# Alternating PSUM banks and a second room for pair sums in the gate units of a hybrid attention block

## The chip, the cores and the metric

The kernel runs on one core of a Trainium2 chip. The metric is the device time of one execution in microseconds. A profiled execution also gives the span from the first to the last instruction of the program, with every instruction on the five engines: PE (matrix products), DVE (vector), ACT (scalar and activation functions), POOL, and SP, which only issues transfers here.

## The reference

One block, 256 tokens, width 2048, all in fp32. Cut to what matters here:

```python
h = rmsnorm(x, g_mix)
proj = h @ w_in                         # 2048 x 10240
q_sb, k_sb, v_sb, q_ca, k_ca, v_ca, gate_sb, gate_ca = split(proj)
y_sb = stick_breaking_attention(q_sb, k_sb, v_sb)     # 8 heads of 128
y_ca = chunked_relpos_attention(q_ca, k_ca, v_ca, rel_bias)   # 8 heads of 128
merged = sigmoid(gate_sb) * (y_sb @ w_sb_out) + sigmoid(gate_ca) * (y_ca @ w_ca_out)
x = x + merged @ w_mix_out
g, u = split(rmsnorm(x, g_ffn) @ w_ffn_in)
x = x + (silu(g) * u) @ w_ffn_out
x = x + sigmoid(rmsnorm(x, g_ple) @ w_ple_gate) * (p @ w_ple_in)
out = rmsnorm(x, g_final)
```

## The kernel before

**Products in three parts.** Every fp32 operand is split into a rounded part hi and a rest lo = value - hi. A product is the sum of hi x hi, hi x lo and lo x hi, three matrix instructions (lines 276 to 278, function `three`). A weight piece of 256 x 512 comes from memory by one transfer into a place `raw` (five places, `RAW = 5`), ACT casts it to hi (L247), DVE subtracts to get lo (all subtractions are recorded at L229, in `minus`). hi and lo have three buffers each, and a fourth in some stages (`four_buffers`).

**Units.** The function `unit` computes two column blocks of 512 (a double group) over 16 rows of weight tiles. A part of its work goes by a Strassen-like scheme: a pair of row tiles of both blocks, seven triple products in place of eight. For it, DVE forms three more weight matrices `xf` (two from raw, one over it, one more: three different lines of `split_pair`, all at L229), ACT casts the two raw pieces (L262, L265) and xf (L268, into `room`), and DVE subtracts (into lo and `room`). `room` is one tile of 128 x 3072 for hi and lo of xf. The pairs are row pairs 2, 4 and 6 of eight, so a unit is 13 pieces: ten single pieces of 12 products and three pairs of 21. The products go into eight PSUM banks: four main sums (`mm`, one for each block and half of the tokens) and four sums of the pairs (`su`, q1, q5, q6, q7). After the last pair, `mid` writes the four sums into SBUF (an ACT copy at L812, four DVE additions at L814), and after the last pieces `add_sums` adds the main sums (L818).

**Gate units.** In the attention part there are five such units (`gate_unit`): the second half of the values of the first mixer with the first gate block, both halves of the values of the second mixer, and three units of gate blocks. They have `alone=True`: main sums always in the pool `ps_mm` (four banks of 512), pair sums always in the attention pool (two tiles of 1024, the function `aux`), which is also where the attention steps have their scores zp, bt, yp.

**Order.** Pieces are worked off one after another by `flush`; `prefetch` issues loads while places are free and splits up to three pieces ahead. Attention work stands in a queue of tasks: for two heads the steps s1 (scores, exponentials), s2 (sums, weights) and s3 (values). `flush(every)` runs one task after each `every` pieces; in a unit with `hold` no task runs from the first to the last pair. Queries and keys (`queries_and_keys`) are groups of four pieces of 16 products (L354, L356); their two sums leave PSUM through `halves` (ACT copy tm L418, DVE addition sm L420). The program is then put into order per engine by a scheduler, and each engine runs its list in order.

The sequence is: first half of the values and one gate block; queries and keys of mixer 0, half 0; first gate unit (`flush(2)`); queries and keys (0, 1) and (1, 0); the other four gate units (`flush(1000)`); queries and keys (1, 1); output projections, mixing, feed-forward, last gate.

Of the kernel before, what the change touches and what calls it, by code (L numbers as in the profile page):

```python
# [9 lines left out]
F32 = mybir.dt.float32  # L10
# [26 lines left out]
MIX_PAIRS = (4, 6)  # L37
RAW = 5
# [5 lines left out]
def block_kernel(ctx: ExitStack, tc: tile.TileContext, x, p, w_in, w_sb_out, w_ca_out, w_mix_out,  # L44
# [95 lines left out]
    pieces = []  # L140
    tasks = deque()
# [22 lines left out]
    def unit(wsrc, n0s, kts, lhs, forms, ext, slots, mid, post, needs, row0=0, pairs=PAIRS, alone=False, after=None,  # L164
             hold=False):
# [8 lines left out]
        taken = [j for j in pairs if j < len(kts) // 2 - 1]  # L174
        for i in range(len(kts) // 2):
# [4 lines left out]
            if i in taken:  # L180
                pieces.append(dict(pc, src=src, pair=True, first=i == taken[0], last=i == taken[-1]))
            else:
                for b in range(2):
                    pieces.append(dict(pc, src=[src[b]], block=b, first=i == 0, last=2 * i + 2 == len(kts)))
# [5 lines left out]
    def load_piece(src, ncol):  # L190
        state["ring"] += 1
        if state["more"] is not None and state["ring"] % (RAW + MORE) in (0, RAW // 2 + 1):
            raw = state["more"]()
        else:
            raw = wp.tile([P, 1024], F32, tag="raw", name="raw", bufs=RAW)
        n = src.shape[1] * ncol
        return raw[:, :n], raw[:, :n].rearrange("p (k n) -> p k n", n=ncol)

# [32 lines left out]
    def split(pc):  # L231
# [4 lines left out]
        state["raw"] -= len(raws)  # L236
        if pc["g"]["kind"] == "unit" and len(raws) == 2:
            return split_pair(pc, *raws)
# [44 lines left out]
    def pair_products(pc):  # L283
# [25 lines left out]
        if z:  # L309
            g["mid"](g)  # L310
            state["hold"] = False

    def products(pc):
# [3 lines left out]
        elif g["kind"] == "unit":  # L317
            if pc["first"]:
                g["ps"] = g.get("ps", []) + [late["ps"][g["pool"]].tile([P, 512], F32, tag="mm", name=f"mm{t}") for t in range(2)]
# [6 lines left out]
            if pc["last"]:  # L326
                g["post"](g, pc["block"])
        elif pc is pieces[1]:
# [34 lines left out]
    state = dict(loaded=0, split=0, at=0, raw=0, hl=0, ext=0, ps=ps_mm, fourth=None, ring=0, more=None, hold=False)  # L363
# [6 lines left out]
    def prefetch():  # L370
        while state["loaded"] < len(pieces) and state["raw"] + len(pieces[state["loaded"]]["src"]) <= RAW + (MORE if state["more"] is not None else 0):
            load(pieces[state["loaded"]])
            state["loaded"] += 1
# [24 lines left out]
    def flush(every=1, until=None, in_turn=False):  # L398

        n = 0  # L400
        while state["at"] < len(pieces) and (until is None or until not in done):
# [5 lines left out]
            if tasks and not state["hold"] and int(n / every) > int((n - 1) / every):  # L407
# [7 lines left out]
    def halves(ps, pool):  # L415

        tm = pool.tile([P, S], F32, tag="tm", name="tm", bufs=2)
        nc.scalar.copy(tm, ps[:, S:])  # L418
        sm = pool.tile([P, S], F32, tag="sm", name="sm", bufs=2)
# [198 lines left out]
    gates = ap.tile([P, NT, 2, D], F32, tag="gates", name="gates", bufs=1)  # L618

# [98 lines left out]
    def ca_tasks(qT, kT, v, h0):  # L718
# [5 lines left out]
        def s1(h):  # L724
            bias = ap.tile([P, 2, 256], F32, tag="bias", name="bias")
# [120 lines left out]
    F_gate = [FP[:, 0], FP[:, 1], room[:, 3072:].rearrange("p (c f s) -> p c f s", c=2, f=4)]  # L846
    work = mp.tile([P, 1024], F32, tag="v1", name="work")
    state["work"] = lambda name: work[:, :512] if name == "af" else work[:, 512:]
    for i, pair in enumerate(PAIRS):
# [6 lines left out]
              add_values((0, 1)), True)  # L856
    flush(2)
# [10 lines left out]
              add_values((1, 0), (1, 1)), True)  # L868
    for c in range(1, 4):
        gate_unit([6 * W + m * D + c * NB for m in range(2)], lambda c=c: gate_slots(c), add_sums, True)  # L870
    flush(1000)
# [103 lines left out]
    state["more"] = lambda: lp.tile([P, 1024], F32, tag="raw", name="raw", bufs=MORE)  # L975
# [190 lines left out]
```

## Time and profile before

| | us |
|---|---|
| median of three runs | 1473.09 (1472.67 to 1473.83) |
| the profiled execution | 1474.41 |
| its span | 1472.7 |
| PE busy | 1452.7 |
| DVE busy | 1242.6 |
| ACT busy | 820.4 |

A matrix instruction is shown from the start of its reading to a modelled end, so neighbours overlap: of 128 x 512 they start 0.23 us apart and are shown as 0.39. An engine's idle time ahead of an instruction is put down to the one whose end released it. The granted clock is given as a share of the full one.

### The profile page before, as it was taken

How to read it: one execution, taken by the hardware profiler on the slowest of the kernel's cores; microseconds unless marked ns; L12 is line 12 of the kernel's file. 1: busy time of each engine (PE TensorE's matmuls, PEld its weight loads, DVE VectorE, ACT ScalarE, POOL GpSimd, SP SyncE). 2: the span in 40 equal slices, each digit the busy share in tenths (PEclk: the TensorE clock that was granted, in tenths of full speed). 3: DMA queues.
4: the chain of work that ended last, by engine and by line, in shares of the span. 5: the costliest groups of instructions: out<-in, count | busy, mean ns of one | idle time of the engine just before them, and what ended most of it. 6: DMA issues, size and time to landing. Idle time of an engine off the chain costs nothing.

```text
span 1472.7 us, 18664 instructions
## 1 busy us (share of the span) xinstructions
PE 1452.7 (99%) x6849; PEld 1211.8 (82%) x6849; DVE 1242.6 (84%) x1570; ACT 820.4 (56%) x967; POOL 23.0 (2%) x44
## 2 busy tenths in 40 slices
PE   9999999989999999999999999999999999999997
PEld 7887788868888888888888888888888888888886
DVE  6868766888886767898999999899999999999775
ACT  6546656556555544555555545556554556565552
POOL 0200000000000000000000000000000000000000
PEclk9999999999999999999999999999999999999999
DMA  9765455556676556765666666666666666656671
GB/s 320 260 205 172 153 183 168 182 165 207 200 232 204 167 171 183 221 211 172 188 201 199 186 216 198 200 213 187 201 198 201 204 188 207 214 188 213 229 230 69
DMA packets 164731, 291.17 MB, mean 198 GB/s; under 512 B 9024, under 2 KB 42096, under 8 KB 164384
## 3 DMA queue, kind: packets, MB, share of 16 engines
q1 hardware_dynamic: 162528, 281.32, 61.5%
q0 software_dynamic: 2112, 8.68, 1.7%
q8 instruction: 53, 0.87, 0.3%
q14 instruction: 38, 0.31, 0.1%
HBM read 284.19 MB, written 5.77 MB: 197 GB/s over the span
## 4 chain that ended last, share of the span: by engine, by line
PE 94%; ACT 2%; DVE 2%; DMA 1%; issue 1%; DVEq 0%; SPq 0%; ACTq 0%
PE mm L277 22%; PE mm L278 22%; PE mm L276 22%; PE mm L354 7%; PE su L277 4%; PE su L278 4%; PE su L276 4%; PE mm L356 4%; PE tp L443 1%; DVE lo L229 1%; ACT hi L247 1%; DMA raw<-in_w_in 1%; DMA raw<-in_w_ple_in 0%; PE mm L344 0%; DVE room L229 0%
## 5 line engine op out<-in xcount | busy, mean ns | idle before, releaser
L229 DVE TENSOR_TENSOR lo<-raw,hi 128x1024 fp32r<-128x1024 f32 (+1 forms) x517 | 626.4, 1219 | 139.9 <-ACT hi L247 125.1
L247 ACT CAST hi<-raw 128x1024 fp32r<-128x1024 f32 (+1 forms) x387 | 404.7, 1050 | 394.8 <-PE mm L278 294.7
L277 PE MATMUL mm<-lo,T 128*128 128x512 f32 x1349 | 527.0, 391 | 0.2 <-DVE lo L229 0.2
L278 PE MATMUL mm<-hi,T 128*128 128x512 f32 x1349 | 522.9, 390 | 0.0
L276 PE MATMUL mm<-hi,T 128*128 128x512 f32 x1349 | 498.7, 392 | 5.6 <-DVE v L818 3.6
L276 PEld LDWEIGHTS mm<-hi,T 128*128 128x128 f32 x1349 | 253.2, 188 | 59.3 <-issue 4.0
L277 PEld LDWEIGHTS mm<-lo,T 128*128 128x128 f32 x1349 | 253.7, 188 | 53.0 <-DVE lo L229 1.0
L278 PEld LDWEIGHTS mm<-hi,T 128*128 128x128 f32 x1349 | 253.7, 188 | 52.3
L354 PE MATMUL mm<-T,hi 128*128 128x512 f32 x512 | 180.0, 398 | 1.6 <-ACT hi L247 1.6
L356 PE MATMUL mm<-T,lo 128*128 128x256 f32 x512 | 140.0, 280 | 0.0
L265 ACT CAST hi<-raw 128x1024 fp32r<-128x1024 f32 x65 | 68.6, 1055 | 85.8 <-DVE raw L229 31.4
L354 PEld LDWEIGHTS mm<-T,hi 128*128 128x128 f32 x512 | 94.8, 188 | 23.0 <-ACT hi L247 2.3
L356 PEld LDWEIGHTS mm<-T,lo 128*128 128x128 f32 x512 | 96.4, 189 | 1.9
L229 DVE TENSOR_TENSOR xf<-raw 128x512 f32<-128x512 f32 x130 | 89.2, 686 | 8.9 <-DMA raw<-in_w_in 2.9
L229 DVE TENSOR_TENSOR T<-xf,T 128x1536 fp32r<-128x1536 f32 x50 | 87.8, 1755 | 7.5 <-ACT T L268 7.4
L262 ACT CAST hi<-raw 128x1024 fp32r<-128x1024 f32 x65 | 68.5, 1053 | 34.6 <-PE mm L278 28.6
L268 ACT CAST T<-xf 128x1536 fp32r<-128x1536 f32 x50 | 74.0, 1479 | 7.4 <-DVE xf L229 6.8
L814 DVE TENSOR_TENSOR C<-su,C 128x512 f32<-128x512 f32 x72 | 47.7, 684 | 0.3
L818 DVE TENSOR_TENSOR C<-mm,C 128x512 f32<-128x512 f32 x72 | 46.8, 683 | 0.0
L229 DVE TENSOR_TENSOR xf<-raw,xf 128x512 f32<-128x512 f32 x65 | 44.6, 686 | 0.4
L229 DVE TENSOR_TENSOR raw<-raw 128x512 f32<-128x512 f32 x65 | 44.5, 685 | 0.2
L229 DVE TENSOR_TENSOR room<-xf,room 128x1536 fp32r<-128x1536 f32 x15 | 26.4, 1757 | 11.2 <-ACT room L268 11.2
(320 smaller groups left out, 1486.5 us busy)
## 6 DMA issues: line engine op xcount, KB each, us to landing
raw<-in_w_ffn_in SPq DMA_DIRECT2D x176, 512.0 KB, 3.9
raw<-in_w_in SPq DMA_DIRECT2D x160, 512.0 KB, 4.2
raw<-in_w_ffn_out SPq DMA_DIRECT2D x88, 512.0 KB, 4.5
raw<-in_w_mix_out SPq DMA_DIRECT2D x32, 512.0 KB, 4.6
raw<-in_w_ple_gate SPq DMA_DIRECT2D x32, 512.0 KB, 4.9
raw<-in_w_sb_out SPq DMA_DIRECT2D x16, 512.0 KB, 3.8
raw<-in_w_ca_out SPq DMA_DIRECT2D x16, 512.0 KB, 3.8
x<-in_x SPq DMA_DIRECT2D x4, 512.0 KB, 10.1
```

Source lines behind the costliest of these rows:

```text
L229: return nc.vector.tensor_tensor(out, a, b, ALU.subtract)
L247: state["cast"] = nc.scalar.copy(hi[:, c : c + m], raw[:, c : c + m])
L262: nc.scalar.copy(h1, raw1)
L265: nc.scalar.copy(h2, raw2)
L268: nc.scalar.copy(xh, xf)
L276: nc.tensor.matmul(ps, xh, hi, start=a, stop=False)
L277: nc.tensor.matmul(ps, xh, lo, start=False, stop=False)
L278: state["mm"] = nc.tensor.matmul(ps, xl, hi, start=False, stop=z)
L354: nc.tensor.matmul(ps, hi[:, i, f], lhs[:, kt, :, :].rearrange("p c s -> p (c s)"), start=a, stop=False)
L356: nc.tensor.matmul(ps[:, :S], lo[:, i, f], lhs[:, kt, 0, :], start=False, stop=z)
L814: nc.vector.tensor_tensor(C[i], q, C[j], ALU.add)
L818: nc.vector.tensor_tensor(g["C"][i], g["ps"][i], g["C"][i], ALU.add)
```

## The change

The change has four parts, all in the attention part.

- A second room. The pair sums of the gate units alternate between `room` and the upper half of T2 (`later_y`), which holds the second mixer's attention results only later.
- Banks exchanged. `alone` is now a pool number that alternates from gate unit to gate unit, beginning with 1. In units of pool 1 (the first, third and fifth) the main sums are in the attention tiles and the pair sums in `ps_mm`; in units of pool 0 as before. The function `banks` hands them out.
- Tasks held. In a gate unit `hold` is set from the first piece to the last, and `flush(None)` runs no task.
- A sixth raw place from the start of the attention part to the output projections. Its 4 KB come from `tm`, `sm` and `bias`, which go from two buffers to one. `held` remembers which places are taken, so that the sixth is used in turn.

`GATE_ORDER` writes the order of the 13 pieces out; it is the order that `unit` had.

```diff
+GATE_PAIRS = (2, 4, 6)
+GATE_ORDER = (0, 0, 1, 1, -2, 3, 3, -4, 5, 5, -6, 7, 7)
...
+def banks(g, pool, name, n):
+    if g["hold"] and pool == 1:
+        return [t[:, o : o + 512] for t in (aux(name) for _ in range(n // 2)) for o in (0, 512)]
+    return [late["ps"][pool].tile([P, 512], F32, tag="mm", name=f"{name}{t}") for t in range(n)]
...
-        if not alone:
+        if alone is None:
             state["unit"] = state.get("unit", -1) + 1
-        pool = 0 if alone else state["unit"] % 2
+        pool = state["unit"] % 2 if alone is None else alone
...
-                 side=None if alone else 1 - pool, hold=hold)
+                 side=1 - pool, hold=alone is not None)
...
-        if state["more"] is not None and state["ring"] % (RAW + MORE) in (0, RAW // 2 + 1):
+        more = held.count(True) < state["places"] and (
+            held.count(False) == RAW or state["ring"] % (RAW + state["places"]) in (0, RAW // 2 + 1)[: state["places"]])
+        held.append(more)
+        if more:
             raw = state["more"]()
...
-            state["hold"] = g["hold"]
-            if g["side"] is None:
-                su = [aux(f"su{i}") for i in range(2)]
-                g["sums"] = [t[:, o : o + 512] for t in su for o in (0, 512)]
-            else:
-                g["sums"] = [late["ps"][g["side"]].tile([P, 512], F32, tag="mm", name=f"su{i}") for i in range(4)]
+            g["sums"] = banks(g, g["side"], "su", 4)
...
-            state["hold"] = False
...
             if pc["first"]:
-                g["ps"] = g.get("ps", []) + [late["ps"][g["pool"]].tile([P, 512], F32, tag="mm", name=f"mm{t}") for t in range(2)]
+                state["hold"] = g["hold"]
+                g["ps"] = g.get("ps", []) + banks(g, g["pool"], "mm", 2)
...
             if pc["last"]:
                 g["post"](g, pc["block"])
+                state["hold"] = g["hold"] and pc["block"] == 0
...
-            if tasks and not state["hold"] and int(n / every) > int((n - 1) / every):
+            if tasks and every and not state["hold"] and int(n / every) > int((n - 1) / every):
...
-        tm = pool.tile([P, S], F32, tag="tm", name="tm", bufs=2)
+        tm = pool.tile([P, S], F32, tag="tm", name="tm", bufs=1)
-        sm = pool.tile([P, S], F32, tag="sm", name="sm", bufs=2)
+        sm = pool.tile([P, S], F32, tag="sm", name="sm", bufs=1)
...
+    more_places(lambda: ap.tile([P, 1024], F32, tag="raw", name="raw", bufs=1), 1)
...
-            bias = ap.tile([P, 2, 256], F32, tag="bias", name="bias")
+            bias = ap.tile([P, 2, 256], F32, tag="bias", name="bias", bufs=1)
...
-    def gate_unit(n0s, slots, post, hold):
-        unit(w2, n0s, range(KD), T1, lambda kt: F_gate[kt // 4 - 1], [room[:, :3072]], slots, mid, post, hneed,
-             alone=True, hold=hold)
+    def gate_unit(n0s, slots, post):
+        pool = state["gate"] = 1 - state.get("gate", 0)
+        unit(w2, n0s, range(KD), T1, lambda kt: F_gate[GATE_PAIRS.index(kt // 2)], [room[:, :3072], later_y[:, :3072]],
+             slots, mid, post, hneed, alone=pool, order=GATE_ORDER)
...
+    later_y = T2.rearrange("p k c s -> p (k c s)")[:, KD * S :]
...
-    flush(2)
+    flush(None)
...
-    flush(1000)
+    flush(None)
...
+        state["places"] = 0
         flush(2.67 if m == 0 else 1)
```

How the change moves instructions is seen at three places. The lines of the changed kernel are higher: L229 is L250, L247 is L270, L559 is L578, L692 and L693 are L712 and L713, L814 and L818 are L834 and L838, L887 is L909, L608 is L627, L651 and L652 are L671 and L672.

The first is DVE at the start of the first gate unit; zp are the scores of the first two heads, raw_1174 (before) and raw_1146 (now) the first raw piece of the unit's first pair, xf its sums. Before:

```order
L625 TENSOR_TENSOR kT_686<-sm_1105,rbc_87 128x256
L692 SCALAR_TENSOR_TENSOR ls_1127<-zp_1114,e_1123 128x768
L229 TENSOR_TENSOR lo_1209<-raw_1174,hi_1208 128x1024
L693 SCALAR_TENSOR_TENSOR e_1123<-zp_1114,e_1123 128x768
L229 TENSOR_TENSOR room_683<-xf_1207,room_683 128x1536
```

Now:

```order
L712 SCALAR_TENSOR_TENSOR ls_1127<-zp_1114,e_1123 128x768
L645 TENSOR_TENSOR kT_686<-sm_1105,rbc_87 128x256
L250 TENSOR_TENSOR lo_1200<-raw_1146,hi_1199 128x1024
L713 SCALAR_TENSOR_TENSOR e_1123<-zp_1114,e_1123 128x768
L250 TENSOR_TENSOR T2_72<-xf_1198,T2_72 128x1536
```

The row of kT now stands behind the first zp row, and the first pair's rest goes into T2; zp's bank is now wanted by the unit's main sums.

The second is ACT at the end of the first gate unit; v and gates are where `mid` and `add_sums` write, zp_1468 and e_1477 belong to the step s1 of the next two heads. Before:

```order
L812 COPY v_1440<-su0_1277 128x512
L247 CAST hi_1520<-raw_1508 128x1024
L247 CAST hi_1524<-raw_1510 128x1024
L559 ACTIVATE v_1440<-v_1440,r1_mix_89 128x512
L688 ACTIVATE e_1477<-zp_1468 128x768
L559 ACTIVATE v_1440<-v_1440,r1_mix_89 128x512
L689 ACTIVATE e_1477<-e_1477 128x768
L887 ACT_TABLE_LOAD
L887 ACTIVATE gates_518<-gates_518,r1_mix_89 128x512
L690 ACT_TABLE_LOAD
L690 ACTIVATE e_1477<-e_1477 128x768
L887 ACT_TABLE_LOAD
```

Now:

```order
L832 COPY v_1412<-su0_1247 128x512
L270 CAST hi_1462<-raw_1450 128x1024
L270 CAST hi_1136<-raw_1305 128x1024
L270 CAST hi_1466<-raw_1452 128x1024
L270 CAST hi_1470<-raw_1454 128x1024
L578 ACTIVATE v_1412<-v_1412,r1_mix_89 128x512 x2
L909 ACT_TABLE_LOAD
L909 ACTIVATE gates_518<-gates_518,r1_mix_89 128x512 x2
L270 CAST hi_1498<-raw_1456 128x1024
```

The three steps of e with their tables have left this place; casts and one table load are what remains.

The third is DVE at the change from the second to the third gate unit; su_2561 and su_2562 are the two tiles of pair sums, mm0_2472 (before) and mm0_2476 (now) a main sum, and xf is the first pair of the third unit. Before:

```order
L229 TENSOR_TENSOR lo_2449<-raw_2707,hi_2448 128x1024
L814 TENSOR_TENSOR v_2733<-su1_2562,v_2732 128x512
L229 TENSOR_TENSOR xf_2821<-raw_2765 128x512
L814 TENSOR_TENSOR v_2732<-su1_2562,v_2733 128x512
L818 TENSOR_TENSOR v_2732<-mm0_2472,v_2732 128x512
L229 TENSOR_TENSOR raw_2765<-raw_2765,raw_2763 128x512
L229 TENSOR_TENSOR lo_2770<-raw_2689,hi_2769 128x1024
L814 TENSOR_TENSOR v_2733<-su0_2561,v_2732 128x512
L814 TENSOR_TENSOR v_2733<-su0_2561,v_2733 128x512
```

Now:

```order
L250 TENSOR_TENSOR xf_2823<-raw_2741 128x512
L250 TENSOR_TENSOR raw_2741<-raw_2741,raw_2739 128x512
L250 TENSOR_TENSOR xf_2823<-raw_2741 128x512
L250 TENSOR_TENSOR xf_2823<-raw_2739,xf_2823 128x512
L834 TENSOR_TENSOR v_2733<-su_2562,v_2732 128x512
L834 TENSOR_TENSOR v_2732<-su_2562,v_2733 128x512
L838 TENSOR_TENSOR v_2732<-mm0_2476,v_2732 128x512
L834 TENSOR_TENSOR v_2733<-su_2561,v_2732 128x512
L834 TENSOR_TENSOR v_2733<-su_2561,v_2733 128x512
```

The whole of the pair's xf now stands ahead of the additions, and the five additions follow each other. Before, the third unit's first products needed the bank of mm0_2472; now they need the tile su_2561. On PE nine products stand between the last into su_2562 and the third unit's first.

More of the change, by code (lines that the diff above doesn't have):

```diff
@@ L140, in block_kernel @@
     pieces = []
+    held = deque()
     tasks = deque()
@@ L162, in group, with unit @@
             ))
-    def unit(wsrc, n0s, kts, lhs, forms, ext, slots, mid, post, needs, row0=0, pairs=PAIRS, alone=False, after=None,
-             hold=False):
-        if not alone:
+    def unit(wsrc, n0s, kts, lhs, forms, ext, slots, mid, post, needs, row0=0, pairs=PAIRS, alone=None, after=None,
+             order=None):
+        if alone is None:
             state["unit"] = state.get("unit", -1) + 1
-        pool = 0 if alone else state["unit"] % 2
+        pool = state["unit"] % 2 if alone is None else alone
         g = dict(kind="unit", post=post, mid=mid, slots=slots, after=after, lhs=lhs, keep=None, forms=forms, ext=ext, pool=pool,
-                 side=None if alone else 1 - pool, hold=hold)
+                 side=1 - pool, hold=alone is not None)
         kts = list(kts)
-        taken = [j for j in pairs if j < len(kts) // 2 - 1]
-        for i in range(len(kts) // 2):
+        if order is None:
+            order = [j for i in range(len(kts) // 2) for j in ([-i] if i in pairs and i < len(kts) // 2 - 1 else [i, i])]
+        taken = [-i for i in order if i < 0]
+        begun = set()
+        for i in order:
+            own = i < 0
+            i = abs(i)
             part = kts[2 * i : 2 * i + 2]
@@ L236, in split @@
         state["raw"] -= len(raws)
+        for _ in raws:
+            held.popleft()
         if pc["g"]["kind"] == "unit" and len(raws) == 2:
@@ L361, in group_products @@
             g["ps"] = None
-    state = dict(loaded=0, split=0, at=0, raw=0, hl=0, ext=0, ps=ps_mm, fourth=None, ring=0, more=None, hold=False)
+    state = dict(loaded=0, split=0, at=0, raw=0, hl=0, ext=0, ps=ps_mm, fourth=None, ring=0, places=0, hold=False)
     late = dict(ps=[ps_mm])
@@ L370, in prefetch @@
     def prefetch():
-        while state["loaded"] < len(pieces) and state["raw"] + len(pieces[state["loaded"]]["src"]) <= RAW + (MORE if state["more"] is not None else 0):
+        while state["loaded"] < len(pieces) and state["raw"] + len(pieces[state["loaded"]]["src"]) <= RAW + state["places"]:
             load(pieces[state["loaded"]])
```

21 lines of the change are left out of this document (12 added, 9 removed).

## The prediction

> **What bounds the kernel now.** I began with the busy shares on the page, then cut the span into stages, then asked in each stage what PE waited for. PE is the bound:
>
> ```profile
> PE 1452.7 (99%) x6849; PEld 1211.8 (82%) x6849; DVE 1242.6 (84%) x1570; ACT 820.4 (56%) x967; POOL 23.0 (2%) x44
> ```
>
> The change touches only the attention part of the program, so the second view is the busy time by stage. 113 us is the end of the first queries and keys, 113 to 176 the first gate unit, 176 to 255 the next queries and keys, 255 to 434 the end of these and the four other gate units:
>
> ```profile
> core 0: us, PE busy (x) PEld busy (x) DVE busy (x) ACT busy (x) POOL busy (x), PEclk, DMA share, GB/s
> 113.00:176.00 63.00, 58.71 (x275) 46.39 (x275) 48.97 (x62) 42.78 (x48) 0.00 (x0) 1.00 0.51 157
> 176.00:255.00 79.00, 79.00 (x468) 69.61 (x467) 56.09 (x80) 45.45 (x62) 0.00 (x0) 1.00 0.59 182
> 255.00:320.00 65.00, 60.03 (x269) 48.26 (x268) 52.73 (x65) 37.79 (x44) 0.00 (x0) 0.97 0.56 176
> 320.00:434.00 114.00, 114.00 (x505) 94.42 (x504) 98.41 (x103) 67.55 (x67) 0.00 (x0) 1.00 0.65 199
> 434.00:1460.00 1026.00, 1026.00 (x4756) 855.77 (x4755) 899.09 (x1124) 561.06 (x655) 11.51 (x18) 1.00 0.64 197
> ```
>
> PE has no idle time except in the first and third of these rows: 63.00 - 58.71 = 4.3 us and 65.00 - 60.03 = 5.0 us. That is where anything can be won. The waits of PE in these two stretches, 110 to 180 and 255 to 320:
>
> ```profile
> PE mm L354 <- ACT hi L247: 1.6, 2, 1.3
> PE mm L276 <- ACT hi L247: 1.1, 1, 1.1
> PE su L277 <- DVE room L229: 1.1, 1, 1.1
> PE mm L277 <- DVE lo L229: 0.3, 2, 0.2
> PE su L276 <- ACT room L268: 0.2, 1, 0.2
> ...
> PE mm L276 <- DVE v L818: 3.6, 1, 3.6
> PE mm L276 <- ACT hi L247: 0.9, 1, 0.9
> PE su L277 <- DVE room L229: 0.4, 1, 0.4
> ```
>
> The idle time understates the loss. Products start 0.23 us apart though each is shown as 0.39 us long, and the longest wait shows what else goes:
>
> ```profile
> 308.80 0.39 PE L277 MATMUL mm<-lo,T 128*128 128x512 f32 x1
> 309.02 0.39 PE L278 MATMUL mm<-hi,T 128*128 128x512 f32 x1
> 312.98 0.47 PE L276 MATMUL mm<-hi,T 128*128 128x512 f32 x1 [3.57 <-DVE v L818]
> ...
> 313.99 0.61 PE L277 MATMUL mm<-lo,T 128*128 128x512 f32 x1
> 314.39 0.63 PE L278 MATMUL mm<-hi,T 128*128 128x512 f32 x1
> ...
> 317.38 0.41 PE L276 MATMUL mm<-hi,T 128*128 128x512 f32 x1
> ...
> 301.81 0.47 PE L276 MATMUL mm<-hi,T 128*128 128x512 f32 x1
> 302.33 0.50 PE L277 MATMUL mm<-lo,room 128*128 128x512 f32 x1
> 302.67 0.40 PE L278 MATMUL mm<-hi,room 128*128 128x512 f32 x1
> ```
>
> Start to start, the wait at 309 cost 3.96 - 0.23 = 3.7 us. The eight products from 313.99 to 317.38 took 3.39 us where 8 x 0.23 = 1.8 would do, so the slow clock behind it cost 1.6 more. A wait that shows no idle (301.81) cost 0.29 and its restart 0.11. So each of the ten waits counted above costs 0.16 (0.39 - 0.23) and 0.11 more than its idle: 9.3 + 2.7 + 1.6, and about 0.9 for three delays like that at 301.81 (estimate: the other two, at 136.97 and 155.87, taken as alike). In all 14.5 us, 6.8 in the first stretch and 7.7 in the second. This is the most that the change can win here.
>
> **The change part by part.** By the order of instructions, PE, DVE and SP issue as many as before and ACT one table load less. Nothing is saved in work; what moves are waits. Durations for all that follows, from the stretch 320 to 430 in which units follow each other without a wait, then ACT and DVE around the two long waits:
>
> ```profile
> L229 DVE TENSOR_TENSOR lo<-raw,hi 128x1024 fp32r<-128x1024 f32 x43 | 52.5, 1221 | 7.3 <-ACT hi L247 4.4 <-ACT hi L262 1.3 <-ACT hi L265 1.3
> L229 DVE TENSOR_TENSOR room<-xf,room 128x1536 fp32r<-128x1536 f32 x9 | 15.8, 1759 | 7.6 <-ACT room L268 7.6
> L814 DVE TENSOR_TENSOR gates<-su,gates 128x512 f32<-128x512 f32 x8 | 5.3, 686 | 0.5 <-PE su L278 0.4
> ...
> 114.35 0.38 ACT L418 COPY tm<-mm 128x256 f32<-128x256 f32 x1
> 114.66 0.82 ACT L688 ACTIVATE e<-zp 128x768 f32<-128x768 f32 x1
> 115.49 1.28 ACT L689 ACT_TABLE_LOAD   x1
> 116.78 0.85 ACT L689 ACTIVATE e<-e 128x768 f32<-128x768 f32 x1
> 117.65 1.28 ACT L690 ACT_TABLE_LOAD   x1
> 118.95 0.85 ACT L690 ACTIVATE e<-e 128x768 f32<-128x768 f32 x1
> 119.70 1.03 ACT L262 CAST hi<-raw 128x1024 fp32r<-128x1024 f32 x1
> ...
> 309.69 0.68 DVE L814 TENSOR_TENSOR v<-su,v 128x512 f32<-128x512 f32 x1
> 310.94 0.69 DVE L229 TENSOR_TENSOR xf<-raw 128x512 f32<-128x512 f32 x1 [0.56 <-DMA raw<-in_w_in]
> 311.55 0.68 DVE L814 TENSOR_TENSOR v<-su,v 128x512 f32<-128x512 f32 x1
> 312.15 0.68 DVE L818 TENSOR_TENSOR v<-mm,v 128x512 f32<-128x512 f32 x1
> ```
>
> *Tasks held, and banks exchanged, in the first unit.* The attention steps s2, s3 and s1 leave the first unit for the queries and keys behind it. There DVE has 79 - 56.1 = 22.9 us free and ACT 33.6; the steps bring DVE some 9 and ACT some 11 us (estimate: the 128x768 rows at about 0.9, two table loads of 1.28, the rest below 0.7 each), and PE waits nowhere in that row. Cost 0; without that cover it would be the 1.3 us that such a clump of ACT costs at the unit's end now. Inside the unit DVE has per unit 3 pairs x (4 x 0.69 + 2 x 1.22 + 1.76) + 10 x 1.22 + 8 x 0.69 = 38.6 us against PE's (10 x 12 + 3 x 21) x 0.2275 = 41.6. With the steps gone it fits, and with two rooms the next pair's sums need not wait for PE to leave the one room. So the waits from 130 to 176 go.
>
> The unit's start stays, and becomes dearer. Its main sums now take the attention banks, and one of them still holds zp until DVE's second zp addition (L693 before, L713 after). I laid the rows behind each other in the new order, from the end of zp, 114.37: PE has 24 products, to 119.9. ACT does the same six rows as above, with the second tm copy inside, so that Ln ends at 120.05, then hi of the pair until 121.0. DVE's lo of that pair follows kT and ends at 122.5, the second addition at 123.4. PE then goes on after 31 products at 123.8, where it could have been at 121.5: 2.3 us. Lower end 1.0 (the cast of the pair alone late), upper end 3.5 (the second transfer of the pair late as well, as the waits of 0.6 above). I take 2.4. First stretch: 6.8 - 2.4 = 4.4 won.
>
> *Second room and sixth raw place, second stretch.* The waits on room and its neighbours there (0.4 and 0.29, with their 0.27 and 0.11, and two of 0.1) go: 1.3 won. The sixth place issues a transfer one piece, about 2.7 us of products, earlier:
>
> ```profile
> raw<-in_w_in SPq DMA_DIRECT2D x160, 512.0 KB, 4.2
> ```
>
> That takes the 0.56 at 310.94 away. The start of the second unit (0.9 idle, 1.2 in all) keeps its chain: cast, table load, Exp, then the cast that PE needs stand on ACT in the same order. I take 1.3 again, ends 0.5 and 2.6.
>
> *Banks exchanged, change from the second to the third unit.* Before, the third unit's first products waited for L818, with a lo, a wait for DMA and two L814 ahead of it on DVE. After, they take the banks of the four sums and need the last of four L814, with one L818 between. Nine products stand on PE between the last product into the sums and the new unit: 2.0 us. Five DVE instructions at 0.60 (311.55 to 312.15) to 0.69, and some 0.15 each for the two hand-overs by the gaps between rows (estimate), are 3.3 to 3.7. The wait is 1.3 to 1.7; I take 1.6 in place of 3.7, and the slow clock (1.6) and its restart go with the short wait: 3.8 won. Lower end 0.9; upper end 3.6, if the pair's transfer is late again. Behind these DVE instructions stand room and lo of the third unit's first pair, which PE needs 27 products (6.1 us) later; 1.76 + 1.22 fit. At the two later changes PE has 24 to 42 products (5.4 to 9.5 us) against some 5.3 us of DVE; 0 to 1.7 each, I take 0.3 each, 0.6 lost, since DVE is at 86% (98.41 of 114) there.
>
> *Single tm, sm and bias.* The second tm copy of a group waits for the first sm addition. tm is 0.38 and PE's next group has other banks, so I cost it at 0; the cover is the free time of the second stage row.
>
> The sum: 4.4 + 1.3 - 0.1 + 3.8 - 0.6 = 8.8, of which I drop 0.2 for rounding of the small waits: 8.6 us. The profiled execution has 1472.7 of span and takes 1474.41 in all; it would become 1464.1 of span. The median of the runs, 1473.09, is 1.3 below the profiled time, and I predict against it: 1473.1 - 8.6 = 1464.5.
>
> [...] Only the gap of 3.57 us was followed by slow products; with those of 1.3 and 1.1 the granted clock stayed at 1.00 (row 113 to 176). [...]
>
> **The rivals.**
> *B, the waits at the changes of units stay.* Had DVE still to do a late pair there, the wait from 309 would be 3.6 and slow the clock: 1.6 + 2.0 less, and 1.5 at a later change: 8.6 - 5.1 = 3.5 won, 1469.6. For it: DVE's 86%, and the four sums that must all be added. Against: the transfer that was late then comes earlier.
> *C, all covered.* Nothing of the 14.5 is left: 1458.6. Against it: zp is still held at the first unit's start.
> *D, nothing measurable.* DVE, 48.97 of 63 and 52.73 of 65, would set the pace, and waits only change place: 1473. For it: the instructions are the same. Against: DVE itself idles for ACT and rooms while PE waits.
> *E, slower.* tm and sm with one buffer tie ACT to DVE: behind a lo of 1.22 and an sm of 0.42 ACT stands 1.6 us, 16 times. It decides once ACT is later than a piece of a group (2.8 us) with its three buffers; then 16 x 0.8 = 13 us come (half of the stand seen by PE, estimate), less 8.6: 1477. Against: no PE wait between 176 and 255. [...]
>
> **How the numbers follow.** Forecast (1460.5 to 1468.5, from the ends above: start 1.0 to 3.5, change 0.9 to 3.6, second start 0.5 to 2.6) 0.58; B (to 1471) 0.15; C 0.08; D 0.10; E 0.09. A difference of 0.2%, 2.9 us, is about what a measurement of this kernel can tell from no change. Faster than 1470.1: forecast, C and most of B, 0.77. Within 0.2%: D and the rest of B, 0.14; slower, E, 0.09. The range 1459.5 to 1473.0 leaves out half of C, a part of D and E. The likeliest case alone has 1460.5 to 1468.5.
>
> **What would show it.** In the new profile: no wait on room or on L354's cast between 130 and 180; one or two waits near 120 to 124, of 1 to 3.5 us together; one at the change near 305 of about 1.5 with the clock at 1.00; PE's idle in the two stretches at 4 or less. Wrong would be: a new wait on tm, sm or L814 of over 3 us, PE idle between 176 and 255, or losses behind 434.

## The result, and the profile after

The changed kernel takes 1463.48 us (median of nine runs, 1462.98 to 1473.24); the kernel before, run beside it, 1473.83 (1472.07 to 1475.04). The ratio estimated over all runs is 0.9938 (the two medians alone give 0.9930), with a 95% interval of 0.9928 to 0.9949: 7.5 to 10.6 us won. The highest of the nine runs, 1473.24, had a mean granted clock of 0.995; the other eight had 0.997 to 0.999 and lie below 1465.3. Predicted were 1464.5 us. The profiled execution took 1464.04 us, with a span of 1462.3.

First line of the page of the changed kernel, busy time by engine:

```profile
PE 1447.8 (99%) x6849; PEld 1210.3 (83%) x6849; DVE 1242.2 (85%) x1570; ACT 819.6 (56%) x966; POOL 22.5 (2%) x44
```

As many PE instructions as before, and 4.9 us less shown as busy. The same table by stage as in the prediction, for the changed kernel; the later stages begin earlier by about what was won:

```profile
113.00:176.00 63.00, 60.20 (x289) 49.66 (x288) 51.80 (x63) 39.95 (x43) 0.00 (x0) 1.00 0.55 173
176.00:250.00 74.00, 74.00 (x447) 65.50 (x446) 53.76 (x78) 47.56 (x63) 0.00 (x0) 1.00 0.56 168
250.00:313.00 63.00, 61.71 (x290) 51.22 (x290) 57.11 (x68) 40.99 (x46) 0.00 (x0) 1.00 0.58 177
313.00:424.00 111.00, 111.00 (x491) 91.94 (x490) 96.48 (x103) 64.19 (x64) 1.55 (x3) 1.00 0.70 212
```

PE's idle time in the first and third row is 2.8 and 1.3 us, where it was 4.3 and 5.0, and the clock is 1.00 in all rows (0.97 in the third before). What PE waited for between 110 and 320 us, now four waits in all:

```profile
PE mm L299 <- ACT hi L270: 1.3, 1, 1.3
PE mm L300 <- DVE lo L250: 1.2, 1, 1.2
PE su L299 <- ACT hi L285: 0.8, 1, 0.8
PE su L300 <- DVE lo L250: 0.8, 1, 0.8
```

The last three stand at the first unit's start, the first at the second unit's. With 0.27 us for each wait, as in the prediction, they cost 3.6 and 1.6 us: of the 14.5 us that were lost, 5.2 are left, 9.3 won. A second way to the same number: two places with equally many products ahead of them, the first product of the first queries and the first product of a late zp. First the kernel before, then the changed one:

```profile
68.48 0.39 PE L354 MATMUL mm<-T,hi 128*128 128x512 f32 x1
...
473.09 0.28 PE L657 MATMUL zp<-sh 128*128 128x256 f32 x1
```

```profile
67.63 0.39 PE L373 MATMUL mm<-T,hi 128*128 128x512 f32 x1
...
462.06 0.28 PE L677 MATMUL zp<-sh 128*128 128x256 f32 x1
```

The distance between the two is 404.61 us before and 394.43 now: 10.2 us won between them. 0.85 us came ahead of them, where the change does nothing (this place lay between 67.0 and 68.6 us in the kernels below, with the same code ahead of it), and 0.6 was lost behind. Between 9.3 and 10.2, 0.9 us is not traced to a row.

### The profile page after: what moved, and what is told of

Read it like the earlier page. It is cut to its first block, busy times and chain, and to the rows that moved or that the text cites. A ratio compares the mean times of both kernels' runs of the same rounds, so it can differ in the third digit from the quotient of the medians.

```text
span 1462.3 us, 18695 instructions
## 1 busy us (share of the span) xinstructions
PE 1447.8 (99%) x6849; PEld 1210.3 (83%) x6849; DVE 1242.2 (85%) x1570; ACT 819.6 (56%) x966; POOL 22.5 (2%) x44
## 4 chain that ended last, share of the span: by engine, by line
PE 96%; DMA 2%; ACT 1%; DVE 1%; issue 0%; SPq 0%; DVEq 0%; ACTq 0%
PE mm L300 23%; PE mm L301 23%; PE mm L299 23%; PE mm L373 8%; PE su L300 4%; PE su L301 4%; PE su L299 4%; PE mm L375 4%; PE tp L462 1%; DMA raw<-in_w_in 1%; DMA raw<-in_w_ple_in 1%; ACT hi L270 0%; DMA raw<-in_w_mix_out 0%; DVE lo L250 0%; PE yp L689 0%
## 5 line engine op out<-in xcount | busy, mean ns | idle before, releaser
L250 DVE TENSOR_TENSOR lo<-raw,hi 128x1024 fp32r<-128x1024 f32 (+1 forms) x517 | 625.7, 1218 | 131.1 <-ACT hi L270 120.8
L270 ACT CAST hi<-raw 128x1024 fp32r<-128x1024 f32 (+1 forms) x387 | 405.1, 1050 | 399.3 <-PE mm L301 299.0
L250 DVE TENSOR_TENSOR T<-xf,T 128x1536 fp32r<-128x1536 f32 x58 | 101.7, 1754 | 10.4 <-ACT T L291 10.4
L250 DVE TENSOR_TENSOR xf<-raw 128x512 f32<-128x512 f32 x130 | 89.1, 685 | 14.9 <-DMA raw<-in_w_ffn_in 4.2
L291 ACT CAST T<-xf 128x1536 fp32r<-128x1536 f32 x58 | 85.9, 1480 | 18.8 <-DVE xf L250 18.1
L285 ACT CAST hi<-raw 128x1024 fp32r<-128x1024 f32 x65 | 68.5, 1053 | 31.5 <-PE mm L301 24.9
L834 DVE TENSOR_TENSOR C<-su,C 128x512 f32<-128x512 f32 x72 | 47.6, 682 | 0.3
L838 DVE TENSOR_TENSOR C<-mm,C 128x512 f32<-128x512 f32 x72 | 46.6, 680 | 0.0
L250 DVE TENSOR_TENSOR xf<-raw,xf 128x512 f32<-128x512 f32 x65 | 44.5, 685 | 0.4
L250 DVE TENSOR_TENSOR raw<-raw 128x512 f32<-128x512 f32 x65 | 44.5, 684 | 0.2
L301 PE MATMUL mm<-T,T 128*128 128x512 f32 (+1 forms) x90 | 33.4, 371 | 0.0
```

Source lines behind the costliest of these rows:

```text
L250: return nc.vector.tensor_tensor(out, a, b, ALU.subtract)
L270: state["cast"] = nc.scalar.copy(hi[:, c : c + m], raw[:, c : c + m])
L285: nc.scalar.copy(h1, raw1)
L291: nc.scalar.copy(xh, xf)
L301: state["mm"] = nc.tensor.matmul(ps, xl, hi, start=False, stop=z)
L834: nc.vector.tensor_tensor(C[i], q, C[j], ALU.add)
```

## The experiments

Each kernel ran in five rounds beside the kernel before. The interval of a ratio is about 0.0013 to either side, 1.9 us, so the time alone tells two of these kernels apart from some 3 us on; for less, the waits in the profile carry the reading. The column "stretch" is the time between the two places above in each kernel's profile; it leaves out what the program's head adds by chance, but not what the clock does. The last column says what the clock does there: one minus the granted clock, times the time, added up over the stretch in steps of 4 us. It is 0 or 1.7, and 8.5 in run 4. Where the text below gives a stretch "without the clock", this loss is taken off it. A profile is one execution; in how many of the others of a kernel the clock fell is not known, so the times may hold more or less of it.

| kernel | median us | ratio to before (interval) | stretch us | of it lost to the clock, us |
|---|---|---|---|---|
| before | 1473.83 | | 404.61 | 1.7 |
| changed kernel | 1463.48 | 0.9938 (0.9928 to 0.9949) | 394.43 | 0 |
| 1 five places, two buffers | 1461.35 | 0.9919 (0.9905 to 0.9932) | 392.55 | 0 |
| 2 one room | 1467.30 | 0.9955 (0.9942 to 0.9967) | 398.71 | 1.7 |
| 3 banks fixed, 0 0 0 0 0 | 1464.79 | 0.9939 (0.9926 to 0.9951) | 396.18 | 1.7 |
| 4 tasks in the first unit, banks 0 1 0 1 0 | 1477.64 | 1.0026 (1.0015 to 1.0036) | 409.14 | 8.5 |
| 5 five places, single buffers | 1465.86 | 0.9944 (0.9932 to 0.9957) | 396.48 | 1.7 |
| 6 other tile for the third unit | 1464.18 | 0.9939 (0.9925 to 0.9952) | 394.28 | 0 |
| 7 five places, two buffers, banks 0 0 1 0 1 | 1459.35 | 0.9904 (0.9891 to 0.9918) | 390.60 | 0 |
| 8 five places, two buffers, late scores | 1464.19 | 0.9938 (0.9926 to 0.9951) | 394.90 | 0 |
| 9 banks 0 0 1 0 1 | 1460.91 | 0.9915 (0.9902 to 0.9929) | 392.24 | 0 |
| 10 banks 0 0 1 0 1, tasks in the first unit | 1466.84 | 0.9953 (0.9941 to 0.9966) | 399.43 | 1.7 |
| 11 before, with single buffers | 1475.28 | 1.0012 (1.0003 to 1.0020) | 404.11 | 0 |
| 12 five places, two tm, single sm and bias | 1464.22 | 0.9935 (0.9922 to 0.9949) | 394.16 | 0 |

**1. Five places, two buffers.**

```diff
-    more_places(lambda: ap.tile([P, 1024], F32, tag="raw", name="raw", bufs=1), 1)
-        tm = pool.tile([P, S], F32, tag="tm", name="tm", bufs=1)
+        tm = pool.tile([P, S], F32, tag="tm", name="tm", bufs=2)
```

(sm and bias alike.)

> The changed kernel without its sixth raw place; tm, sm and bias have two buffers again. Theory P (the places only took away the 0.56 us wait for a transfer in front of the change to the third unit, and single tm, sm and bias cost nothing): 1463.5 to 1464.5 us, against 1463.5 for the changed kernel, PE's waits as in it (3.6 us at the first unit's start, 1.6 at the second's, none at the change near 303) or up to 1 us more. Theory R (an early transfer of the third unit's first pair is what took the wait at the change away): a wait of DVE's additions of 2 to 3.6 us near 303 comes back, 1466 to 1469. Rival E of the prediction (single tm and sm cost time): faster than the changed kernel, 1461 or less.

Measured 1461.35, 2.1 us below the changed kernel (1.9 in the stretch; the intervals of the two ratios overlap by 0.0004). So the fourth part of the change seems to take time, not to bring any. The start of the first unit shows where. First DVE and ACT of the changed kernel there:

```profile
113.05 0.69 DVE L250 TENSOR_TENSOR xf<-raw 128x512 f32<-128x512 f32 x1 [3.62 <-DMA raw<-in_w_in]
...
115.40 0.42 DVE L439 TENSOR_TENSOR sm<-mm,tm 128x256 f32<-128x256 f32 x1
...
115.85 0.37 ACT L437 COPY tm<-mm 128x256 f32<-128x256 f32 x1 [1.26 <-DVE sm L439]
...
116.67 1.22 DVE L250 TENSOR_TENSOR lo<-raw,hi 128x1024 fp32r<-128x1024 f32 x1
...
120.44 1.03 ACT L285 CAST hi<-raw 128x1024 fp32r<-128x1024 f32 x1
```

DVE stands 3.62 us for a transfer of the first pair, with the first unit's lo and the sm of the last queries and keys queued behind that xf. The lo at 116.67, which PE needs, ends late (1.2 us of wait at 117.94). The second tm copy has only the one buffer and stands 1.26 us for the first sm; Exp, Ln and the pair's cast (L285) are queued behind it on ACT. The same with five places and two buffers:

```profile
112.73 0.69 DVE L250 TENSOR_TENSOR xf<-raw 128x512 f32<-128x512 f32 x1 [1.12 <-DMA raw<-in_w_in]
...
113.05 0.38 ACT L437 COPY tm<-mm 128x256 f32<-128x256 f32 x1
...
118.40 1.03 ACT L285 CAST hi<-raw 128x1024 fp32r<-128x1024 f32 x1
```

DVE stands 1.1 us, the tm copy not at all, and the cast comes 2.0 us earlier (1.6 counted from the start of the stretch, which lies 0.44 earlier in this kernel). The transfer itself is not later in the changed kernel: xf begins 45.4 us after the start of the stretch there and 45.5 here. What differs is the order: with six places DVE does the unit's lo behind that xf, here ahead of it. PE waits 0.7 and 0.5 us here instead of 2.8 in all. Theory P falls; the mechanism of rival E in the prediction is there.

**2. One room.**

```diff
-        unit(w2, n0s, range(KD), T1, lambda kt: F_gate[GATE_PAIRS.index(kt // 2)], [room[:, :3072], later_y[:, :3072]],
+        unit(w2, n0s, range(KD), T1, lambda kt: F_gate[GATE_PAIRS.index(kt // 2)], [room[:, :3072]],
```

> The changed kernel with one room for the pair sums, as before. Theory P: the waits on room come back in the first two units, 1.1 + 0.4 us of idle with their restarts, 1.5 to 2.5 in all, and nothing else: 1465 to 1466. Theory R (a room is only waited for where the attention steps delay DVE): no wait on room, 1463.5. Third possibility: the first pair of the third unit is late too for want of a room, and the wait at the change comes back: 1467 to 1469.

Measured 1467.30, 3.8 us above the changed kernel. PE's waits from 110 to 320, the two that are new:

```profile
PE mm L299 <- DVE v L834: 1.7, 1, 1.7
...
PE su L300 <- DVE room L250: 0.6, 1, 0.6
```

A wait on room comes back, and also one for the additions at the change to the third unit: the third possibility. So the second room is worth more than the 1.3 us that it shared with the sixth place in the sum. In this execution the clock adds something too, 1.7 us; without it the stretch is 2.6 longer than the changed kernel's, still twice the 1.3. The same pair of waits at the first unit's start (0.80 and 0.79 us) is in both kernels; the stretch behind it with one room, then the stretch around it in the changed kernel (the column ahead of the last two is the granted clock):

```profile
121.50:126.00 4.50, 3.92 (x10) 3.11 (x11) 4.50 (x6) 3.11 (x4) 0.00 (x0) 0.62 0.41 120
```

```profile
118.00:126.00 8.00, 6.41 (x26) 4.66 (x27) 6.25 (x9) 6.82 (x7) 0.00 (x0) 1.00 0.46 132
```

**3. Banks fixed.**

```diff
-        pool = state["gate"] = 1 - state.get("gate", 0)
+        pool = 0
```

> The changed kernel with main sums always in the pool of four banks and pair sums always in the attention tiles, as before. Theory P (the exchange is what removes the wait at the change from the second to the third unit, and it makes the first unit's start dearer because zp holds a tile): the wait of about 3.7 us with the slow clock (1.6) comes back near 305, and the 3.6 us at the first unit's start shrink to 0 to 2: 1465 to 1469. Theory R (places and room removed the wait at the change): no wait there, and the start cheaper: 1460 to 1463.5.

Measured 1464.79, 0.2 below theory P's range. Two of PE's waits from 110 to 320:

```profile
PE mm L300 <- DVE lo L250: 2.3, 2, 2.0
...
PE mm L299 <- DVE v L838: 0.2, 1, 0.2
```

At the change to the third unit PE first waits 0.2 us for L838 and seven products later 2.0 us for a lo of that unit, which now stands on DVE behind the additions and a row of 1.75 us; products 0.43 us apart follow, the slow clock. The first unit's start is cheap. The price of the exchange alone stands between this run and run 9, whose first unit has the same banks: 1464.79 - 1460.91 = 3.9 us (3.9 in the stretch too). Of it 1.7 is the clock in run 3's profile and 2.2 the waits. That is near the prediction's 3.8 for the change of units, but by luck: the prediction had a wait of 3.7 shrink to 1.6, here one of 2.3 goes to nothing. The intervals of the two ratios overlap a little (0.9926 to 0.9951, 0.9902 to 0.9929).

**4 and 10. Tasks in the first unit.** `early` is true for the first unit, which then holds the tasks from its first pair to the last only.

```diff
+            state["hold"] = g["hold"]
+            g["sums"] = banks(g, g["side"], "su", 4)
...
+            state["hold"] = g["hold"] and not g["early"]
...
-    flush(None)
+    flush(2)
```

> The changed kernel with the attention tasks in the first unit as before: a task after each second piece, held only between the first and the last pair, main sums of this unit in the pool of four banks (then exchanged from unit to unit). Theory P (the steps inside the unit made the waits between 130 and 176): some 5 of the 6.8 us come back there less the 3.6 of the start that go: 1464.5 to 1467. Theory R (second room and sixth place take these waits away by themselves): 1460 to 1463.

Measured 1477.64, slower than the kernel before, which neither theory had. Two waits of PE between 261 and 273 us, at the second unit's start, carry it, the 4.7 of the first row and the 3.7 of the second, with the slow clock beside them (8.5 us in the table; the mean granted clock of this execution is 0.993, of the changed kernel's 0.998):

```profile
PE bt L723 <- ACT sh L673: 5.4, 2, 4.7
PE yp L679 <- ACT sh L673: 3.7, 1, 3.7
```

In this kernel the banks were 0 1 0 1 0, so the second unit's main sums wanted the attention tiles while the last steps of the heads (bt, yp) still needed them. That is a fault of the experiment. Run 10 asks again with 0 0 1 0 1, beside run 9; the banks are all that differs from run 4, and these waits are gone there.

> As the run before (banks 0, 0, 1, 0, 1), but with the attention tasks running in the first unit, as before the change: the clean price of holding them, without the tile that the tasks and the second unit's main sums shared in the earlier run. Theory P: the first stretch is 6 us longer than in the run before (waits near 126, 137 and 171, once with a slow clock), nothing else changes, 1466 to 1468. Theory R (holding the tasks only shifts the waits to the queries and keys and to the second unit): within 2 us of the run before, 1461 to 1463.

Measured 1466.84 against 1460.91 of run 9, 5.9 us, intervals apart (0.9941 to 0.9966, 0.9902 to 0.9929): theory P. Two of its waits, the first for the most part at 174 us, where the kernel before waited too, the second at 129, where that one waited 0.2 us:

```profile
PE mm L375 <- ACT hi L270: 1.6, 2, 1.4
PE mm L300 <- DVE lo L250: 1.0, 1, 1.0
```

Behind the second the clock fell (granted clock 0.83 from 124 to 133 us). Without that 1.7 the stretches of runs 10 and 9 differ by 5.5 us: theory P still, with the slow clock that it named as a part.

**9. Banks 0 0 1 0 1.**

```diff
-        pool = state["gate"] = 1 - state.get("gate", 0)
+        state["gate"] = state.get("gate", -1) + 1
+        pool = (0, 0, 1, 0, 1)[state["gate"]]
```

> The changed kernel (six places, single tm, sm and bias) with the banks 0, 0, 1, 0, 1 instead of 1, 0, 1, 0, 1: the first unit's main sums leave zp's tile alone. Theory T1 (the 3.6 us at the first unit's start come from that tile, as the prediction's step says, which put 2.3 on it): the first stretch is 2.5 to 3.2 us shorter, as with fixed banks, and the change near 300 has no wait: 1460.3 to 1461.5. Theory T2 (the banks of the second unit, which now follow those of the first without an exchange, bring a wait of 1 us or more at the second unit): 1462 to 1464.

Measured 1460.91, 2.6 us below the changed kernel (2.2 in the stretch): theory T1, by the waits; the intervals of the ratios meet at 0.9928 to 0.9929. From 110 to 320 PE has left:

```profile
PE mm L299 <- ACT hi L270: 1.3, 1, 1.3
PE mm L300 <- DVE lo L250: 0.8, 2, 0.5
```

The second unit's start is as in the changed kernel (1.3), the change near 300 has no wait, and of the 2.8 us at the first unit's start 0.8 stay, at two later lo (128.4 and 131.0 us). Zp's tile had made PE take the first pair ahead of the second block's pieces, and so want the pair's cast and lo 24 products earlier.

**6. Another tile for the third unit.**

```diff
+        if g["hold"] and pool == 1 and name == "mm" and state["gates"] > 1:
+            if "spare" not in g:
+                g["spare"] = [aux(name) for _ in range(2)]
+            t = g["spare"].pop()
+            return [t[:, o : o + 512] for o in (0, 512)]
```

> The changed kernel with the main sums of the third and the fifth gate unit in the attention tile that is freed last instead of first; nothing else, the order of instructions stays. The prediction had taken this tile: four additions and one main addition of DVE in front, a wait of 1.3 to 1.7 us at the change near 303. Theory P (the pool hands out the tile freed first, and that is why no wait is seen): a wait of 1.3 to 1.9 us comes at the change, 0 to 1 at the last change, and the time is 1464.8 to 1466. Theory R (DVE is early enough at this change whatever the tile): no wait, 1463.5.

Measured 1464.18, with the four waits of the changed kernel and no other. It does not decide: in the order of instructions the third unit's first product still waits for the same addition, the second of four, since the two tiles come in the order in which they fall free. The run is a repeat of the changed kernel, 0.7 us from it. A kernel in which this product waits for the last addition was not run.

**5, 12 and 11. What the single buffers cost.**

```diff
-    more_places(lambda: ap.tile([P, 1024], F32, tag="raw", name="raw", bufs=1), 1)
```

> The changed kernel without its sixth place, but with tm, sm and bias still single: it parts the two halves of the fourth part. Theory P' (the sixth place puts DVE's subtraction of the first pair ahead of other work, where it stands 3.6 us for its transfer; the single tm only passes that delay on to ACT): DVE's stand at the first unit's start is about 1.1 us as with five places, the waits there 1.2 to 2 us in all, and the time 1461 to 1462.2, near that of five places with double buffers (1461.4). Theory E' (the single tm costs the time by itself): 1463 to 1464, with ACT's second tm copy standing about 1.3 us.

Measured 1465.86 (1462.51 to 1467.18): above both theories. Against five places with two buffers it is 4.5 us, the intervals meet at 0.9932 (3.9 in the stretch). In this profile the clock fell too (1.7 us in the table; the two waits at the first unit's start are 1.5 and 0.5 us); without it the stretches are 2.2 apart. So single buffers do cost by themselves, some 2 us, with the clock's 1.7 beside them in this profile. Whether the sixth place wins any of it back is not shown: the intervals of this run and the changed kernel overlap (0.9932 to 0.9957, 0.9928 to 0.9949), and without the clock their stretches are 0.4 us apart. PE's waits, two of four:

```profile
PE mm L299 <- DVE v L833: 1.7, 1, 1.7
PE su L299 <- ACT hi L285: 1.5, 1, 1.5
```

The second one is the chain of run 1 (the tm copy stands 0.69 us). The first is at the change to the third unit, and DVE's rows there show the order of the kernel before, with rows of the new pair between the additions:

```profile
304.00 0.69 DVE L250 TENSOR_TENSOR xf<-raw 128x512 f32<-128x512 f32 x1 [0.57 <-DMA raw<-in_w_in]
304.61 0.69 DVE L833 TENSOR_TENSOR v<-su,v 128x512 f32<-128x512 f32 x1
305.21 0.68 DVE L250 TENSOR_TENSOR raw<-raw 128x512 f32<-128x512 f32 x1
305.81 0.69 DVE L833 TENSOR_TENSOR v<-su,v 128x512 f32<-128x512 f32 x1
```

Run 12 gives tm alone its second buffer back.

> Five places, tm with two buffers, sm and bias single. The order on ACT at the first unit's start is the same with single and double tm; the order on DVE at the change near 303 is that of the single buffers (rows of the next pair between the additions). Theory P: the second tm copy no longer stands for an sm (0.69 us with single tm), so the waits at the first unit's start are those of five places with double buffers (1.2 us of idle), while the wait of about 1.7 us at the change stays: 1463 to 1464.5. Theory R (the place of the rows does not matter, tm alone is the cost): both go, 1461 to 1462. Theory S (sm or bias is the cost at the start): nothing changes against all three single, 1465 to 1467.

Measured 1464.22, and PE's waits are those that theory P named:

```profile
PE mm L299 <- DVE v L833: 1.7, 1, 1.7
PE su L299 <- ACT hi L285: 0.7, 1, 0.7
PE mm L299 <- ACT hi L270: 0.5, 1, 0.5
PE su L300 <- DVE lo L250: 0.5, 1, 0.5
```

The start is repaired (1.5 to 0.7, and the clock stays at 1.00), the change is not. So the single buffers cost in two ways: tm while it runs, and sm or bias by the order that the scheduler makes. Which of these two it is, and why the rows of the pair then stand between the additions, was not looked into; with six places and all three single they do not. Run 11 is the same edit alone in the kernel before.

> The kernel before with nothing but tm, sm and bias with one buffer. The prediction costed this at 0. By the runs with five places (double 1461.4, single 1465.9) it costs 2 to 4.5 us here too: 1475 to 1478, with ACT's second tm copy standing 0.7 us or more for an sm at the first unit's start. If the cost belongs to the order that the scheduler found in the changed kernel alone, the time stays within 1 us: 1472.5 to 1474.5.

Measured 1475.28 against 1473.42, ratio 1.0012 (1.0003 to 1.0020): 0.4 to 2.9 us, at the lower edge of the expectation; its profiled stretch, 404.11 us, is not longer than that of the kernel before (404.61). But this profile is of the fastest of its eleven runs (1472.92), and the clock did not fall in it, as it did in the profile of the kernel before; without that 1.7 its stretch is 1.2 longer. The second tm copy stands 0.82 us for an sm here too. What the other ten lost, at mean granted clocks of 0.995 to 0.998, no row shows.

**7 and 8. Towards a better kernel.** Run 7 joins runs 1 and 9, run 8 joins run 1 and `flush(5)` in place of `flush(4)` ahead of the first unit.

> Five places and double tm, sm, bias; the first gate unit's main sums in the pool of four banks, the second's too, then exchanged (0, 0, 1, 0, 1). Theory T1 (the first unit's waits come from the tile that zp holds, which makes PE take the first pair before the second block): the 1.5 us at the first unit's start fall to 0 to 0.5, the change near 300 stays without a wait, 1459.5 to 1460.8. Theory T2 (ACT's chain for zp stands in front of the cast whatever the bank): waits of 1 us or more stay at the start, 1461 to 1462.

Measured 1459.35 (1458.86 to 1460.18), 4.1 us below the changed kernel, with intervals apart: the fastest here. From 110 to 320 one wait of PE is left, at the second unit's start:

```profile
PE mm L299 <- ACT hi L270: 0.9, 1, 0.9
```

> Five places and double tm, sm, bias; the scores of the first two heads are a task after the first unit instead of ahead of it (one task after each five pieces instead of four in the queries and keys before it). Both theories let the waits at the first unit's start go (1.5 us). Theory T1: nothing comes in its place, since DVE has 20 us free in the next queries and keys: 1459.5 to 1460.5. Theory T3 (the step is dearer there, because all six steps then fall into the next sixteen pieces and the last one ahead of the second unit is squeezed): 1461.5 to 1464 with a new wait between 165 and 200 or a longer one at the second unit's start.

Measured 1464.19: theory T3, 0.2 above its range. The first unit's start is free, but the second's now has the last of the attention steps squeezed in ahead of it, its longest wait being this one:

```profile
PE yp L676 <- ACT sh L670: 1.4, 1, 1.4
```

## Why the prediction was right, and which steps were not

The time came out 1.0 us from the forecast, the sum of the trace 0.7 (8.6 forecast, 9.3 found). That the sum is so near is in part luck, for misses of opposite sign stand in it: the first unit's start cost 1.2 more than taken, the change to the third unit gave 1.5 more, and 0.6 taken off for later changes was not lost.

- *Tasks held.* The waits from 130 to 176 went; the stretch behind took the tasks at no cost (74.00 of 74.00 busy). Runs 9 and 10 put 5.9 us on it, 5.5 by the stretches without the clock; the prediction had 6.8 for all waits there, less the start. Right.
- *The first unit's start.* Taken as 2.4 us (1.0 to 3.5), measured 3.6 in the trace, just above the upper end. The step that zp's tile holds PE up is right, and run 9 prices it at 2.6. What failed is the working behind it: it followed ACT's rows with the second tm copy inside them, but not what that copy itself waits for, nor DVE's 3.62 us for the pair's transfer with a lo behind it; a late transfer stood only in its upper end.
- *Single tm, sm and bias, at 0.* Wrong. The cover named was the free time between 176 and 255; the cost came at the first unit's start and at a change of units, which that cover does not reach. With five places it is 4.5 us by the medians (1461.35 to 1465.86) and 2.2 by the stretches without the clock; the changed kernel, with the sixth place, is 2.1 and 1.9 above run 1. Rival E had the mechanism (ACT standing for an sm), but not its size or place: not sixteen stands of 0.8, but one of 0.7 to 1.3 in front of a chain that PE waits for, and an order changed elsewhere.
- *The change to the third unit, 1.6 us taken.* Wrong by the whole of it; there is no wait. Rows of PE and DVE there, in order of time:

```profile
301.38 0.39 PE L301 MATMUL su<-room 128*128 128x512 f32 x1
...
301.97 1.41 DVE L834 TENSOR_TENSOR v<-su,v 128x512 f32<-128x512 f32 x2
...
303.30 0.68 DVE L838 TENSOR_TENSOR v<-mm,v 128x512 f32<-128x512 f32 x1
...
303.65 0.40 PE L299 MATMUL mm<-hi,T 128*128 128x512 f32 x1
...
303.90 1.28 DVE L834 TENSOR_TENSOR v<-su,v 128x512 f32<-128x512 f32 x2
```

  301.38 is the last product into the pair sums, and 303.65, after the nine products counted, the first of the third unit. DVE's five rows take from 301.97 to 305.18, 3.2 us, close to the 3.3 to 3.7 of the step; what is wrong is which of them PE needs. The third unit starts while the last two additions have not begun: its bank is in the tile su_2562, free after the second addition at 303.38, not in su_2561. The part on the change says su_2561, and that is the mistake. 5.3 us were won here in place of 3.8 (3.7 for the wait, 1.6 for the clock).
- *Room and sixth place, 1.3 won.* The waits went. Run 2 shows the room to be worth more, 3.8 us with a slow clock and 2.6 without, since a pair that waits for a room also makes the additions late; the sixth place is no gain beside what it was paid with.
- *The second unit's start, 1.3 taken.* 1.6 measured. *Later changes, 0.6 lost.* No wait there: 111.00 of 111.00 busy.
- *Idle time of 4 us or less in the two stretches:* 4.1. *A wait of about 1.5 us near 305:* none.
- *The clock.* In the kernel before, only the gap of 3.57 us had slow products behind it (0.43 us apart in place of 0.23), and gaps of 1.3 and 1.1 left the clock at 1.00. That the shorter wait of 1.6 would keep the clock, and so win the 1.6 of the slow products, was the author's estimate from these gaps. The changed kernel agrees (waits up to 1.3 us, clock 1.00). As a bound on the single wait it does not hold: in run 2, 0.80 and 0.79 us, 1.5 us apart, were followed by a granted clock of 0.62.

## What to carry to other kernels

When a bank or buffer changes hands, look up which of the instructions that empty it the new user waits for, and lay the rows out to that one: here the tile that falls free first was handed out, and the wait that was priced at 1.6 us is none. A buffer given up is not free because the engines around it have idle time on average; follow the one instruction that will now stand, and what is queued behind it where an engine in demand is short of cover. And undo each part of a good change by itself: here one part of four cost about 2 us, another choice 2.6, and without both the kernel takes 1459.35 us (run 7).

## What was not expected of the hardware

The clock fell after waits that are short each. With one room, PE's products from 122.55 to 125.54 started 0.43 us apart (granted clock 0.62 from 121.5 to 126):

```profile
120.56 0.50 PE L299 MATMUL su<-hi,T 128*128 128x512 f32 x1 [0.80 <-ACT hi L285]
120.90 0.40 PE L299 MATMUL mm<-hi,T 128*128 128x512 f32 x1
122.08 0.67 PE L300 MATMUL su<-lo,T 128*128 128x512 f32 x1 [0.79 <-DVE lo L250]
122.55 0.63 PE L301 MATMUL su<-hi,T 128*128 128x512 f32 x1
...
125.54 0.46 PE L299 MATMUL mm<-hi,T 128*128 128x512 f32 x1
```

The changed kernel has the same two waits at the same distance without it (clock 1.00, products 0.23 us apart behind them). Run 3 shows the fall behind 2.05 us, and run 5 lost 1.7 us to it with waits of 1.7, 1.5, 0.5 and 0.5, while a single wait of 1.7 (runs 2 and 12) and, in run 11, waits of 2.6 and 1.0 for the additions of L818 left the clock at 1.00. What sets the fall off is not shown by these runs. In run 2 it cost some 1.5 us (seven products 0.20 us late each; 1.7 by the granted clock), so a comparison of 1 or 2 us from one profile needs the clock looked at first.
